# Seven block products instead of eight in the gate and up projections of a two-layer encoder

## The chip, the cores and the metric

The kernel runs on one core of a Trainium2 chip. The metric is the device time of one execution in microseconds (us), and three executions of the kernel before gave 2786.99, 2788.01 and 2792.45 us, so the median is 2788.01 us. A core has a matrix engine (TensorE, in the rows PE, with its weight loads as PEld), three engines for elementwise work (VectorE or DVE, ScalarE or ACT, GpSimd or POOL) and a queue that issues transfers (SyncE or SP).

## The reference

The program computes two layers on 1024 prompt tokens and 64 sample tokens, which the kernel treats as one block of 1088 tokens of width 1024. Layer 0 mixes tokens by attention and a gated recurrence, layer 1 by a convolution and a linear recurrence. Each layer ends with the same feed-forward network, and it is this network that the change touches:

```python
hn = (rms_norm(x, norm_ffn[l]) * (1.0 + sc2) + sh2).astype(x.dtype)
x = x + ((1.0 + g2) * swiglu(hn, ffn_wg[l], ffn_wu[l], ffn_wd[l])).astype(x.dtype)

def swiglu(h, wg, wu, wd):
    return (jax.nn.silu(h @ wg) * (h @ wu)) @ wd      # 1024 -> 2816 -> 1024
```

`sh2`, `sc2` and `g2` are rows of a matrix product of the conditioning vector with `w_ada` (six rows of 1024 for each layer).

## The kernel before

Features lie on partitions: `x` is 8 tiles of 128 features by 1088 tokens. Every float32 operand of a large product is split into a rounded part `hi` and a remainder `lo` (`split`, L85: ScalarE copies, VectorE or GpSimd subtracts), and a product is the sum of three passes hi·hi, hi·lo and lo·hi. Tokens come in three chunks of 384, 384 and 320 (`CH`).

The feed-forward (`ffn`, L319) runs over 22 blocks of 128 hidden features. For each it multiplies with the gate block and the up block: 8 tiles of K, 3 passes and 3 chunks, so 72 matmuls for each of the two (`gemm_chunk`, L108). ScalarE takes silu of the gate from PSUM, VectorE multiplies it with the up sum (L341), and the result is split and stays on chip. After every two blocks `project` (L300) multiplies them with their rows of `wd` and adds the gated sum into `x` (L313). Gate, up and down products thus alternate, and weights of 128x1024 are loaded and split two at a time through the pool `wp`, which exists for the whole program.

RMSNorm with its shift and scale (`norm_stats`, `norm_apply`, L240 to L276) for the feed-forward is made chunk by chunk behind the last output projection of the mixer (`norm_into`, called `after` chunks of `project`), reads the inverse root from PSUM and leaves `x` as it is. Five of the six conditioning rows of layer 0 are made during the mixer; row 5 of layer 0 and all of layer 1, 56 tiles, are made inside the feed-forward of layer 0 by `ada_tick`, on VectorE, GpSimd and ScalarE (`mods_dve`, L179). In layer 1 the last projection is `finish` (L1116), with the final norm in it.

Where code isn't under an `InOrder` wrapper (all operations of which show line 46), the order on each engine is made by the framework's planner, with `soon()` and `later()` as priorities; a pool's memory is handed on tile by tile (`reuse_waits="tile"`).

## Time and profile before

| | |
|---|---|
| median of three runs | 2788.01 us (2786.99 to 2792.45) |
| profiled execution, first to last instruction | 2788.7 us, 0.7 us above the median |
| PE busy | 2668.2 us, 96% |
| DVE, POOL, ACT busy | 1604.6, 1085.1, 921.5 us (58%, 39%, 33%) |
| feed-forward of layer 0 and 1 begin at about | 826 us and 1970 us |
| transfers | 193.78 MB, 69 GB/s over the span |

The profile is of one execution. Matmuls are pipelined, so that the duration of one is a latency and the rate is read from the distance of the starts. Where a row has "idle before", the engine named after the arrow is what ended the wait.

### The profile page before, as it was taken

To read this page: it belongs to the slowest core of one execution; us is meant where nothing else is said; L and a number is where in the kernel's file an instruction comes from. 1 tells how busy PE (TensorE), PEld (TensorE's weight loads), DVE (VectorE), ACT (ScalarE), POOL (GpSimd) and SP (SyncE) were. 2 spreads that over 40 slices of the span, in tenths; PEclk is the share of its full clock that TensorE was granted. 3 is DMA by queue.
4 is the path that set the end of the run, shared out by engine and by line. 5 is a ranking of instruction groups with operands and counts; after the bars stand their busy time and mean duration, and the time that the engine had idled before them with its cause. 6 is when DMAs were issued, how large, how long until landed. Compare 5 with 4: busy or idle time off the path is not lost.

```text
span 2788.7 us, 39952 instructions
## 1 busy us (share of the span) xinstructions
PE 2668.2 (96%) x16280; PEld 2611.0 (94%) x16280; DVE 1604.6 (58%) x2586; ACT 921.5 (33%) x1712; POOL 1085.1 (39%) x681
## 2 busy tenths in 40 slices
PE   6898999998899999999999999989999999999998
PEld 5898999998789999999999988989999999999997
DVE  8778766667985656643333476678633333333335
ACT  4225344444645333321111165553511111111113
POOL 6446445454645666621222254452512222222223
PEclk9999999999999999999999999999999999999999
DMA  6332111112213444411111102221001111111111
GB/s 241 91 109 89 58 40 55 41 61 106 66 46 121 134 135 130 135 55 46 46 46 41 50 28 73 68 89 48 22 31 46 46 46 46 46 46 46 46 46 65
DMA packets 69399, 193.78 MB, mean 69 GB/s; under 512 B 13280, under 2 KB 24544, under 8 KB 69216
## 3 DMA queue, kind: packets, MB, share of 16 engines
q1 hardware_dynamic: 69216, 191.24, 21.5%
q8 instruction: 128, 2.10, 0.3%
q14 instruction: 55, 0.45, 0.0%
HBM read 173.94 MB, written 17.27 MB: 69 GB/s over the span
## 4 chain that ended last, share of the span: by engine, by line
PE 48%; DVE 8%; ACT 4%; POOL 1%; issue 1%; DVEq 0%; POOLq 0%; ACTq 0%
PE ps_mm L115 29%; PE ps_z L308 8%; PE ps_t L308 8%; DVE xc L46 2%; POOL ada_raw L182 1%; DVE rg L46 1%; DVE mu L46 1%; PE ps_mm L308 1%; DVE junk L185 1%; DVE x L313 1%; ACT rg L46 1%; ACT mu L46 1%; ACT junk L183 1%; PE ps_t L46 0%; PE ps_t L115 0%
## 5 line engine op out<-in xcount | busy, mean ns | idle before, releaser
L115 PE MATMUL ps_mm<-h_hi,w_hi 128*128 128x384 f32 (+1 forms) x2688 | 885.5, 330 | 7.6 <-ACT w_hi L86 3.3
L115 PE MATMUL ps_mm<-h_hi,w_lo 128*128 128x384 f32 (+1 forms) x2688 | 886.5, 330 | 3.6 <-DVE w_lo L87 1.9
L115 PE MATMUL ps_mm<-h_lo,w_hi 128*128 128x384 f32 (+1 forms) x2688 | 886.5, 330 | 1.8 <-DVE h_lo L272 1.1
L87 POOL TENSOR_TENSOR w_lo<-w_raw,w_hi 128x1024 fp32r<-128x1024 f32 x168 | 427.2, 2546 | 1064.8 <-ACT w_hi L86 1012.1
L115 PEld LDWEIGHTS ps_mm<-h_hi,w_hi 128*128 128x128 f32 x2688 | 508.6, 189 | 12.1 <-ACT w_hi L86 4.1
L115 PEld LDWEIGHTS ps_mm<-h_hi,w_lo 128*128 128x128 f32 x2688 | 509.1, 189 | 5.8 <-DVE w_lo L87 2.2
L115 PEld LDWEIGHTS ps_mm<-h_lo,w_hi 128*128 128x128 f32 x2688 | 508.9, 189 | 3.5 <-DVE h_lo L272 1.4
L341 DVE TENSOR_TENSOR sg<-sg,ps_mm 128x384 f32<-128x384 f32 (+1 forms) x128 | 68.0, 531 | 502.5 <-PE ps_mm L115 496.6
L86 ACT CAST w_hi<-w_raw 128x1024 fp32r<-128x1024 f32 x174 | 181.7, 1049 | 276.5 <-PE ps_mm L115 198.0
L313 DVE SCALAR_TENSOR_TENSOR x<-ps_t,mods,x 128x384 f32<-128x384 f32 (+2 forms) x392 | 187.4, 498 | 124.5 <-PE ps_t L308 123.8
L308 PE MATMUL ps_z<-hid,w_hi 128*128 128x384 f32 (+1 forms) x1008 | 247.2, 327 | 0.3 <-DVE x L313 0.3
L308 PE MATMUL ps_t<-hid,w_hi 128*128 128x384 f32 (+1 forms) x1008 | 246.9, 327 | 0.0
L334 ACT ACTIVATE sg<-ps_mm 128x384 f32<-128x384 f32 (+1 forms) x128 | 60.3, 471 | 558.8 <-PE ps_mm L115 558.7
L313 DVE SCALAR_TENSOR_TENSOR x<-ps_z,mods,x 128x384 f32<-128x384 f32 (+2 forms) x396 | 187.4, 494 | 79.8 <-PE ps_z L308 79.5
L87 DVE TENSOR_TENSOR hid<-sg,hid 128x384 fp32r<-128x384 f32 x132 | 179.1, 1358 | 65.3 <-ACT hid L86 64.9
L308 PEld LDWEIGHTS ps_z<-hid,w_hi 128*128 128x128 f32 x1008 | 178.9, 188 | 0.8 <-DVE x L313 0.8
L308 PEld LDWEIGHTS ps_t<-hid,w_hi 128*128 128x128 f32 x1008 | 178.3, 188 | 0.0
L182 POOL TENSOR_TENSOR ada_raw<-ada_raw,cbc 128x1024 f32<-128x1024 f32 x56 | 137.2, 2450 | 92.1 <-DVE junk L185 53.8
L308 PE MATMUL ps_t<-hid,w_lo 128*128 128x384 f32 (+1 forms) x504 | 164.7, 327 | 0.0
L308 PE MATMUL ps_z<-hid,w_lo 128*128 128x384 f32 (+1 forms) x504 | 164.7, 327 | 0.0
L86 ACT CAST hid<-sg 128x384 fp32r<-128x384 f32 x132 | 65.1, 494 | 242.3 <-DVE sg L341 242.2
L185 DVE SCALAR_TENSOR_TENSOR junk<-ada_raw,cbc 128x1024 bf16<-128x1024 f32 x56 | 80.0, 1429 | 89.0 <-ACT junk L183 88.9
(389 smaller groups left out, 4593.7 us busy)
## 6 DMA issues: line engine op xcount, KB each, us to landing
ada_raw<-in_adaT SPq DMA_DIRECT2D x56, 512.0 KB, 3.5
w_raw<-in_wg SPq DMA_DIRECT2D x44, 512.0 KB, 3.6
w_raw<-in_wu SPq DMA_DIRECT2D x44, 512.0 KB, 3.5
w_raw<-in_wd SPq DMA_DIRECT2D x44, 512.0 KB, 3.5
w_raw<-in_w_in_even SPq DMA_DIRECT2D x28, 512.0 KB, 3.7
w_raw<-in_adaT SPq DMA_DIRECT2D x24, 512.0 KB, 3.6
w_raw<-in_w_in_odd SPq DMA_DIRECT2D x16, 512.0 KB, 3.6
o_raw<-o_dram SPq DMA_DIRECT2D x14, 544.0 KB, 3.9
```

Source lines behind the costliest of these rows:

```text
L46: return lambda *a, **k: self.tc.keep_in_program_order(f(*a, **k))
L86: S.copy(hi, src)
L87: (lo_eng or G).tensor_sub(lo, src, hi.bitcast(F32))
L115: PE.matmul(ps[:, :n], a[:, k * P:(k + 1) * P], b[:, c0:c0 + n], start=(i == 0), stop=(i == last))
L182: G.tensor_mul(raw, raw, cb[v])
L183: S.activation(junk(), raw, AF.Identity, accum_out=mods[l][:, t, v:v + 1])
L185: V.scalar_tensor_tensor(junk(), raw, 1.0, cb[v], ALU.mult, ALU.mult, accum_out=mods[l][:, t, v:v + 1])
L308: PE.matmul(ps[:, :n], a[:, m * P:(m + 1) * P], b[:, c0:c0 + n], start=(i == 0), stop=(i == 3 * nk - 1))
L313: V.scalar_tensor_tensor(x[m][:, r0:r0 + rn], ps[:, r0 - c0:r0 - c0 + rn], gate[:, m, b:b + 1], x[m][:, r0:r0 + rn], ALU.mult, ALU.add)
L334: S.activation(sg[ci][:, :n], ps, AF.Silu)
L341: V.tensor_mul(t, t, ps)
```

## The change

For a block of 128 hidden features the weights are seen as a 2x2 matrix of blocks: w11 and w12 are the gate's lower and upper half of K (512 each), w21 and w22 the up projection's. The activations are a 2x2 matrix too: lower and upper half of K by the first and second 544 tokens. Seven products of such blocks (each 4 tiles of K, 3 passes, 2 chunks of 272 tokens) with sums and differences of blocks ahead of and behind them give the four blocks of the result. The seven operands of the activations are made once for a layer (`enter`: `first_ops` and `late_ops`), the sums of the weights for each of the 22 blocks (`weights`).

For these operands to fit, `x` is written to DRAM before it is normalised in place, and read back after the 22 blocks (`unpark`). The hidden blocks go to DRAM one by one and come back in `down_half`, where the down projections run by groups of 2 or 3 blocks after all gate and up products. Conditioning row 5 of layer 0 is made on TensorE in the mixer (`todo_pe`); the 48 tiles of layer 1 are made during the down projections of layer 0. The last output projection of a mixer runs in four chunks of 272 tokens. The pools `wp` and `w2` and the PSUM pool are opened anew for each stage. The core of the diff:

```diff
+HT = NT // 2
+Q = HT // 2
+CH4 = [(0, Q), (HT, Q), (Q, Q), (HT + Q, Q)]
...
+    def enter(l, x, tag, stat_tmp, tmp):
+        ops = [[] for _ in range(7)]
+        def late_ops(j):
+            A, B = slice(j * Q, (j + 1) * Q), slice(HT + j * Q, HT + (j + 1) * Q)
+            for k in range(4):
+                split_at(x[k + 4][:, A], ops[4][k], j, G)
+            for k in range(4):
+                V.tensor_sub(x[k + 4][:, A], x[k + 4][:, A], x[k][:, A])
+                split_at(x[k + 4][:, A], ops[5][k], j, V)
+            for k in range(4):
+                d, c = x[k + 4][:, B], slice(j * Q, (j + 1) * Q)
+                hi, lo = ops[6][k][:, 0, c], ops[6][k][:, 1, c]
+                S.activation(hi, d, AF.Copy, scale=-1.0)
+                V.scalar_tensor_tensor(lo, d, -1.0, hi.bitcast(F32), ALU.mult, ALU.subtract)
+        def first_ops(j):
...
+            for k in range(4):
+                split_at(x[k][:, A], ops[0][k], j, V)
+            for k in range(4):
+                a, b, d = x[k][:, A], x[k][:, B], x[k + 4][:, B]
+                t1 = tmp()[:, :Q]
+                V.tensor_sub(t1, b, a)
+                V.tensor_sub(b, b, d)
+                V.tensor_sub(a, a, b)
+                split_at(a, ops[1][k], j, V)
+                split_at(b, ops[2][k], j, G)
+                split_at(t1, ops[3][k], j, G)
+        def after(ci):
+            c0, n = CH4[ci]
+            r = slice(c0, c0 + n)
+            for k in range(KD):
+                dma(x_dram[k][:, r], x[k][:, r])
+            rs = norm_stats(CH4[ci], x, stat_tmp)
+            kept = tmp()[:, :n]
+            S.copy(kept, rs)
+            for k in range(KD):
+                (G if k in (2, 3, 7) else V).tensor_mul(x[k][:, r], x[k][:, r], kept)
+                for r0, rn, b in rng(c0, n):
+                    v = x[k][:, r0:r0 + rn]
+                    S.activation(v, v, AF.Identity, scale=scale[l][1][:, k, b:b + 1], bias=mods[l][:, 3 * KD + k, b:b + 1])
+            if ci % 2:
+                first_ops(ci // 2)
+        return (ops, late_ops), after
+    def up_half(l, ops_late, t_tag, op_tag):
...
+            layout(fp, ("n22", NT, 4), ("t4", NT, 4), ("b21", NT, 4), ("wg", 1024, 2), ("wu", 1024, 2), ("s1", 512, 1),
+                   ("wh", 512, 5), ("wl", 512, 5))
+            def w_split(src):
...
+                split(src, hi, lo, G)
+                return hi, lo
+            def weights(f):
...
+                with soon():
+                    yield w_split(w11)
+                    V.tensor_add(s1, w21, w22)
+                    V.tensor_add(w21, w11, w21)
+                    V.tensor_add(w11, s1, w11)
+                    yield w_split(w11)
+                    yield w_split(w21)
+                    yield w_split(s1)
+                    yield w_split(w12)
+                    V.tensor_add(w12, w11, w12)
+                    yield w_split(w22)
+                    yield w_split(w12)
+            with soon():
...
+                late_ops(0)
+                late_ops(1)
...
+                for f in range(FF):
+                    X, Y, Z, W = (ap.tile([P, 2, 512], F32, name="acc" + n, tag="acc" + n, bufs=1) for n in "XYZW")
...
+                    def n1():
+                        S.copy(t, x_)
+                    def n6():
+                        V.tensor_sub(t, y_, t)
+                    def p7():
+                        V.tensor_add(hB, z_, t)
+                    def n5():
+                        V.tensor_add(hB, w_, hB)
+                    def n2():
+                        S.activation(g, x_, AF.Silu)
+                    def p4():
+                        V.tensor_add(hA, z_, t)
+                        V.tensor_mul(hA, hA, g)
+                        dma(hid_dram[f][:, :HT], hid[:, :HT])
+                    def p3():
+                        V.tensor_add(t, w_, t)
+                        S.activation(t, t, AF.Silu, scale=-1.0)
+                        V.tensor_mul(hB, hB, t)
+                        dma(hid_dram[f][:, HT:], hid[:, HT:])
+                    steps = list(zip((X, Y, Z, W, X, Z, W), ops, (1, 1, 1, 1, 0, 0, 0), (n1, n6, p7, n5, n2, p4, p3)))
+                    ws = weights(f)
+                    for part in ((steps[:4], steps[4:]) if f == 0 else [[st] for st in steps]):
+                        wt = [next(ws) for _ in part]
+                        for j in range(2):
+                            for w, (acc, op, start, use) in zip(wt, part):
+                                product(acc, w, op, j, start)
+                                if j == 1:
+                                    with soon():
+                                        use()
...
+    GROUPS = (2, 3, 3, 3, 3, 3, 3, 2)
+    def down_half(l, x, fp, t_tag, after=None, last=None, tick=None):
...
+                dma(lo.bitcast(F32), hid_dram[f])
+                with soon():
+                    split(lo.bitcast(F32), hi, lo, V)
+                hs.append((hi, lo))
+                ws.append(load_w(I["wd"][l, f], fp, "wd", bufs=6))
...
+                project(ws, hs, x, mod(l, 5), after if gi == len(GROUPS) - 1 else tick, ("t", "z", "mm"))
...
+                if not todo and todo_pe:
+                    j = todo_pe.pop(0)
+                    raw = raw_tile()
+                    dma(raw, I["ada5"][j])
+                    ps = bank("o")
+                    for e in range(KD):
+                        PE.matmul(ps[:, :2], raw[:, e * P:(e + 1) * P], sc[:, e, :], start=(e == 0), stop=(e == KD - 1))
...
+        todo = [(i, j) for i in range(6) for j in range(KD)]
+        def ada_tick(ci):
+            with later():
+                for n in range(3 if len(todo) > 24 else 2):
...
+                    mods_dve(1, i * KD + j, cb, raw,
+                             lambda: fp.tile([P, 1024], BF16, name="junk", tag="junk"), j % 2 == 0)
```

## Rows read from the trace of the kernel before

**Rows 1.** The page's first part: busy time, share of the span, instructions.

```profile
span 2788.7 us, 39952 instructions
PE 2668.2 (96%) x16280; PEld 2611.0 (94%) x16280; DVE 1604.6 (58%) x2586; ACT 921.5 (33%) x1712; POOL 1085.1 (39%) x681
```

**Rows 2.** Windows: stretch, its length, busy time of PE, PEld, DVE, ACT, POOL; granted clock.

```profile
300.00:500.00 200.00, 197.52 (x1330) 189.43 (x1330) 131.32 (x187) 86.77 (x198) 97.98 (x79) 0.99 0.15 45
...
860.00:1050.00 190.00, 189.86 (x1153) 189.54 (x1152) 111.33 (x171) 72.12 (x118) 118.30 (x48) 1.00 0.45 140
...
2155.00:2724.00 569.00, 569.00 (x3446) 569.00 (x3445) 208.18 (x350) 93.71 (x144) 116.45 (x48) 1.00 0.15 45
```

**Rows 3.** Windows over the two entries: last output projection and first feed-forward block.

```profile
1943.50:2007.50 64.00, 59.55 (x331) 58.16 (x330) 48.62 (x100) 36.22 (x76) 31.53 (x33) 0.89 0.05 17
798.30:855.50 57.20, 52.41 (x304) 50.68 (x305) 47.30 (x96) 34.61 (x75) 36.04 (x36) 0.94 0.16 54
```

**Rows 4.** Chain that ended last, layer 1: start us, us, what.

```profile
2155.45 34.20 PE ps_mm L115 x208
2190.16 7.68 PE ps_mm L115 x48
2226.80 34.20 PE ps_mm L115 x208
```

**Rows 5.** Timeline of PE: the first matmul of three runs of 24.

```profile
2308.46 0.33 PE L115 MATMUL ps_mm<-h_hi,w_hi 128*128 128x384 f32 x1
...
2312.62 0.31 PE L115 MATMUL ps_mm<-h_hi,w_hi 128*128 128x320 f32 x1
...
2316.13 0.34 PE L115 MATMUL ps_mm<-h_hi,w_hi 128*128 128x384 f32 x1
```

**Rows 6.** Timeline of PE in the last projection, 256 columns, 30 matmuls apart.

```profile
2765.94 0.40 PE L46 MATMUL ps_z<-hid,w_hi 128*128 128x256 f32 x2
...
2769.44 0.40 PE L46 MATMUL ps_t<-hid,w_hi 128*128 128x256 f32 x2
```

**Rows 7.** Groups of DVE, feed-forward of layer 1, 2084 to 2724 us.

```profile
L313 DVE SCALAR_TENSOR_TENSOR x<-ps_t,mods,x 128x384 f32<-128x384 f32 x72 | 44.3, 616 | 39.1 <-PE ps_t L308 38.9
...
L87 DVE TENSOR_TENSOR hid<-sg,hid 128x320 fp32r<-128x320 f32 x18 | 43.8, 2433 | 9.5 <-ACT hid L86 9.5
L341 DVE TENSOR_TENSOR sg<-sg,ps_mm 128x384 f32<-128x384 f32 x36 | 20.0, 555 | 247.7 <-PE ps_mm L115 247.7
L313 DVE SCALAR_TENSOR_TENSOR x<-ps_z,mods,x 128x256 f32<-128x256 f32 x35 | 16.9, 484 | 10.1 <-PE ps_z L308 10.1
...
L313 DVE SCALAR_TENSOR_TENSOR x<-ps_t,mods,x 128x64 f32<-128x64 f32 x36 | 9.9, 275 | 0.0
```

**Rows 8.** Groups of POOL and of ACT in the same stretch.

```profile
L87 POOL TENSOR_TENSOR w_lo<-w_raw,w_hi 128x1024 fp32r<-128x1024 f32 x54 | 131.0, 2430 | 510.4 <-ACT w_hi L86 510.3
...
L86 ACT CAST w_hi<-w_raw 128x1024 fp32r<-128x1024 f32 x54 | 56.7, 1050 | 116.1 <-PE ps_mm L115 92.7 <-DMA w_raw<-in_wd 23.4
```

**Rows 9.** Timeline of DVE and of POOL in the entry to layer 1's feed-forward.

```profile
1949.75 0.55 DVE L251 TENSOR_TENSOR ntmp<-ntmp 128x384 f32<-128x384 f32 x1
...
1952.33 0.94 DVE L251 TENSOR_TENSOR ntmp<-ntmp 128x384 f32<-128x384 f32 x1
...
1981.63 0.48 DVE L251 TENSOR_TENSOR ntmp<-ntmp 128x320 f32<-128x320 f32 x1
...
1994.60 2.42 DVE L268 SCALAR_TENSOR_TENSOR ntmp<-x,scale,ps_o 128x256 f32<-128x256 f32 x8 [4.23 <-PE ps_o L230]
...
1952.03 0.83 POOL L248 TENSOR_TENSOR ntmp<-x 128x384 f32<-128x384 f32 x1 [0.29 <-DVE x L313]
...
1967.22 1.01 POOL L253 TENSOR_TENSOR ntmp<-ntmp 128x384 f32<-128x384 f32 x1 [1.62 <-DVE ntmp L251]
```

**Rows 10.** Groups of DVE in that entry, 1943.5 to 2007.5 us.

```profile
L251 DVE TENSOR_TENSOR ntmp<-ntmp 128x384 f32<-128x384 f32 x8 | 5.5, 685 | 0.1
...
L251 DVE TENSOR_TENSOR ntmp<-ntmp 128x320 f32<-128x320 f32 x4 | 3.7, 923 | 0.0
```

**Rows 11.** Timeline of PE in the first mixer: the 16 conditioning products of one tile.

```profile
68.23 1.84 PE L46 MATMUL ps_o<-sc,raw_sc 128*128 128x2 f32 x16
```

**Rows 12.** Groups of DVE in the feed-forward of layer 0, 860 to 1222 us.

```profile
L185 DVE SCALAR_TENSOR_TENSOR junk<-ada_raw,cbc 128x1024 bf16<-128x1024 f32 x56 | 80.0, 1429 | 89.0 <-ACT junk L183 88.9
L87 DVE TENSOR_TENSOR hid<-sg,hid 128x384 fp32r<-128x384 f32 x22 | 35.6, 1618 | 7.5 <-ACT hid L86 7.2
```

**Rows 13.** DMA issues of the page: KB of each, median us from issue to landing.

```profile
w_raw<-in_wd SPq DMA_DIRECT2D x44, 512.0 KB, 3.5
...
o_raw<-o_dram SPq DMA_DIRECT2D x14, 544.0 KB, 3.9
```

More of the change, by code (lines that the diff above doesn't have):

```diff
@@ new lines, in unpark @@
+    def unpark(tag):
+        x = [u(tag, name="x") for _ in range(KD)]
+        for c0, n in CH:
+            for k in range(KD):
+                dma(x[k][:, c0:c0 + n], x_dram[k][:, c0:c0 + n])
+        return x
+    GROUPS = (2, 3, 3, 3, 3, 3, 3, 2)
+    def down_half(l, x, fp, t_tag, after=None, last=None, tick=None):
+        f = 0
+        for gi, size in enumerate(GROUPS):
+            hs, ws = [], []
+            for f in range(f, f + size):
+                if gi == len(GROUPS) - 1:
+                    t = fp.tile([P, 2, NT], F32R, name="hid", tag="hid", bufs=2)
+                    hi, lo = t[:, 0, :], t[:, 1, :]
+                else:
+                    tag = t_tag if f < 2 or f % 2 else "C"
+                    hi, lo = u(tag, F32R, "hid_hi"), u(tag, F32R, "hid_lo")
+                dma(lo.bitcast(F32), hid_dram[f])
[3 more added lines that the diff above has]
+                ws.append(load_w(I["wd"][l, f], fp, "wd", bufs=6))
+            f += 1
+            if gi == len(GROUPS) - 1 and last:
+                last(ws, hs)
+            else:
+                project(ws, hs, x, mod(l, 5), after if gi == len(GROUPS) - 1 else tick, ("t", "z", "mm"))
@@ L366, in hybrid_encoder @@
     o_dram = [dram.tile([P, NT], F32, name=f"o_dram{k}") for k in range(KD)]
+    x_dram = [dram.tile([P, NT], F32, name=f"x_dram{k}") for k in range(KD)]
+    hid_dram = [dram.tile([P, NT], F32, name=f"hid_dram{f}") for f in range(FF)]
     wi = I["w_in_even"]
-    with phase_pool("mix") as mp:
+    banks_open = psum_pool("banks0")
+    with phase_pool("wp") as stage["w"], phase_pool("mix") as mp:
+        masks = mp.tile([P, 6, P], U8, name="masks")
+        causal = mp.tile([P, P], F32, name="causal")
+        strict = mp.tile([P, P], F32, name="strict")
@@ L515, in hybrid_encoder @@
         for i in range(2):
-            w = tuple(wp.tile([P, 1024], F32R, name=nm, tag=nm, bufs=2) for nm in ("w_hi", "w_lo"))
+            w = tuple(stage["w"].tile([P, 1024], F32R, name=nm, tag=nm, bufs=2) for nm in ("w_hi", "w_lo"))
             oS.copy(w[0], wraw[i])
@@ L1049, in bring, with odd_out @@
             outs[j] = hi, lo
-        def odd_out(js, own, aft=None):
+        def odd_out(js, own, aft=None, chunks=CH):
             for j in js:
                 if j not in outs:
-                    bring(j, lambda name, dt=F32: u("A" if name == "o_raw" else "C", dt, name), G)
+                    bring(j, lambda name, dt=F32: u("B" if name == "o_raw" else "C", dt, name), G)
             hs = [outs[j] for j in js]
@@ L1232, in hybrid_encoder @@
         POOL_Y = ((0, 2, 4), (5,), (0, 3, 6))
-        ffn(1, x, box[0], fp, None, 0, 1, finish)
+        x = unpark("B")
+        down_half(1, x, fp, "A", last=finish)
+    stage["open"].close()
 def _layout(i):
```

215 lines of the change are left out of this document (104 added, 111 removed).

## The prediction

> **What bounds the kernel now.** I read the page first, for the share of each engine, then windows by stage, the chain that ended last, the timeline of PE for its rate, the groups of the elementwise engines inside one stage, and last the two places where a mixer hands over to the feed-forward. PE is busy 96% of 2788.7 us [rows 1]. In both feed-forwards it has no gap: 569.00 of 569.00 us in layer 1, at full granted clock (1.00, which is the 2.4 GHz level) [rows 2]. The chain of layer 1 runs on PE alone and repeats every 71.35 us (2155.45 to 2226.80), two hidden blocks with their down products [rows 4]. The reader is to see that in these stages only fewer or shorter matmuls shorten anything: DVE is busy 208 of 569 us, POOL 116 [rows 2]. At the two entries it is otherwise: 64.0 us pass with 59.55 of PE and a clock of 0.89, and 57.2 us with 52.41 and 0.94, while DVE is busy 76% and 83% of them [rows 3].
>
> **The change, part by part.** The sum is made against the profiled execution, 2788.7 us, which is 0.7 us above the median of the runs; I leave that difference in.
>
> *Gate and up products.* A matmul of 384 columns starts 4.16/24 = 0.1733 us after the one before, one of 320 columns 3.51/24 = 0.1463 [rows 5]. One block now is 144 matmuls: 24 x 2 x (2 x 0.1733 + 0.1463) = 23.66 us; two of them and two blocks of down products make 71.0 of the 71.35 seen. After the change it is 7 products x 4 tiles x 3 passes x 2 halves = 168 matmuls of 272 columns. No row has 272. The line through 384 and 320 gives 0.1260; between 320 and the 256 columns of the last projection (30 starts in 3.50 us, 0.1167 [rows 6]) it is 0.1241. I take 0.125: 21.0 us a block. The gain is 2.66 us for each of 44 blocks, 117 us; the ends are 2.49 and 2.81, 110 and 124 us. An eighth of the columns goes, but not an eighth of the time, because 24 more matmuls a block each bring the part that does not go with columns. The row of 256 is 10 ns above 256 columns at 2.4 GHz, those of 320 and 384 are 13 ns above [rows 5, 6]. The Trainium skill (TensorE: Matmul & The Clock Gate, "Wait — 56ns, not 53.3ns?") has 2.5 ns for this part; by it a matmul of 272 would take 115.8 ns, an estimate, and the gain would be larger than mine by 1.5 us a block. These rows show four to five times that, and the measurement decides.
>
> *What must stay behind those products.* A product lasts 3.0 us, a block 21. POOL makes seven remainders of 512 columns, half of 2430 ns each [rows 8]: 8.5 us. ACT has seven copies at half of 1050 ns and three passes of 544 columns: some 6 us. DVE has four sums of 512, near 0.65, and seven passes of 544, near 0.72 (from 0.555 at 384 [rows 7]): 7.6 us, and more by waits for POOL: a subtraction of 320 columns with both inputs in SBUF takes 2433 ns where POOL works, as long as POOL's own 2430 [rows 7, 8]. Six such operations a block with half a POOL operation each add 4 us. All are far under 21, and an accumulator is read at least two products (6 us) before it is written again. So I put the steady state at PE's rate, plus 0.1 us a block for hand-overs, 4 us. If this cover were gone, the next to bind would be DVE.
>
> *The two entries.* This is where I expect most of the gain to go. Before, PE starts on chunk 0 while the norm of later chunks is made. After, the first four products need two of four chunks, the rest all of them, and the elementwise work is larger. For 272 columns I take DVE 0.43 us with two SBUF inputs (0.48 and 0.55 at 320 and 384 [rows 9]), 0.50 from PSUM (0.484 at 256 [rows 7]), POOL 0.64 to 0.75 (0.83 and 1.01 at 384 [rows 9]). DVE for each chunk: 8 additions into x 4.0 (5.6 in the last chunk, whose 208 + 64 columns are two operations, 275 ns at 64 [rows 7]), 5 sums and 5 multiplications 4.3, the power's input 0.15; over four chunks 35.6. `first_ops`: 20 operations twice, 17.2. `late_ops`: 12 twice, 10.4. Together 63 us without a wait, against 48.6 before with waits [rows 3]. Of these 104 have two SBUF inputs and meet POOL, which by its rows has 41 us of its own here and up to 9 more for the weights of block 0. In the entry before, such operations took 685 ns and 923 ns instead of 550 and 480 [rows 9, 10], 0.24 us more at the mean of these twelve. That puts 25 us on DVE; without it DVE has 63, with all of it 88. I take 80, and 3 us for the norm's latency (an idle DVE of 4.23 us stands before the last chunk [rows 9]), 5 for the products left when the last operand comes and 2 for a lower clock: 90 us from the first matmul of the last projection to the end of block 0. The ends are 69 (63, 1 and 5) and 105 (88, 4, 5, and 8 for the clock). Before it was 64.0 and 57.2 [rows 3]; less the 2.7 already counted, 61.3 and 54.5. So the entries cost 29 and 35 more, 64 us in all (22 to 95, and 10 more if the first weights of layer 0 too, whose memory the mixer's last temporaries hold, come late by the load, the copy and the remainder of two, [rows 8, 13]). PE has 45 us of work in such a stretch, so it must idle some 40 us and its clock fall; those at 0.89 and 0.94 [rows 3] show a milder form.
>
> *Conditioning on PE.* A tile's 16 small products take 1.84 us [rows 11], of which the last's tail is hidden by the next matmul; I take 1.75, and eight are 14 us. The mixer's PE is busy 197.5 of 200 us in one stretch [rows 2], so little is hidden: 10 us (4 to 14).
>
> *Hand-overs.* From up to down, weights of the first group wait for memory of the last products: a load of 3.5 us [rows 13] is ahead of time, a remainder of 2.4 us [rows 8] is not; x and hidden blocks (3.9 us for 544 KB [rows 13]) have products in flight as cover. I take 3 us, twice (0 to 6 each). From down to the second mixer the first weights no longer lie in a pool of their own: 3.5 + 1.05 + 2.4 less the norm's tail, 5 us (0 to 8).
>
> *Down projections of layer 0.* PE has 22 x 11.83 = 260 us here. DVE has additions into x, 24 in each of 8 groups, 15.8 us a group, 126; remainders of 22 hidden blocks, 26 clean or up to 55 (1618 ns for 384 in rows where POOL shares [rows 12]); 72 conditioning dots at 1.43 us [rows 12], 103; and three norm chunks at the end. That is 255 to 285 us before the norm. Before, the same dots had 720 us to lie in. Evictions go first, so PE isn't stopped at once, but the rest becomes late and holds the memory and the start of the second mixer. I take 12 us (0 to 35). The down products themselves stay as they are; layer 1 has no dots and hides its remainders.
>
> Sum: -117 + 64 + 10 + 6 + 5 + 12 + 4 = -16 us; 2788.7 - 16 gives 2773 us.
>
> **The rivals.**
> 1. *The entry is mostly hidden.* For it: late operands are asked for early, DVE can work through the last projection, and the planner may pack DVE and POOL apart. Then the entries cost 22 to 35, the down stage little: 2788.7 - 117 + 28 + 20 = 2720, range 2700 to 2745. Against it: DVE is already busy 76 and 83% of the shorter entries.
> 2. *DVE binds outside the products* (slower). Both entries at 105, and the dots of the down stage pushed into the second mixer: -117 + 95 + 14 + 10 + 8 + 30 + 4 = +44, near 2833. It decides from about 80 us of entry cost together with 20 of the down stage. For it: the sums above reach it without a mishap when every SBUF operation waits as it did. Against it: operations that follow on each other on DVE shut POOL out just as well.
> 3. *No gain from seven products.* PE's rate could be set by weight loads, of which there are 168 now for 144, or by the operand chain. If a matmul of 272 took the 0.1463 of 320, a block would take 24.6 us and the time would go up by 40 before all else: 2880. Against it: 256 columns ran at 0.1167, so loads keep that pace [rows 6]. The Trainium skill (the same page, "LDWEIGHTS (loading the stationary operand)") puts a load of 128 columns at 107 ns, an estimate that stays under 125; by that the rate holds.
>
> **How the numbers follow.** Two runs differ by up to 0.2%, so 2782.4 to 2793.6 us is no change. My own case, entry costs between 45 and 85 us, has 0.46, and gives 2745 to 2795; rival 1 has 0.21; rival 2 has 0.28; rival 3 has 0.05. Faster is rival 1 and most of my case: 0.60. Same is the upper end of mine and the lower edge of rival 2: 0.11. Slower: 0.29. The range runs from rival 1's lower end to where rival 2's upper part is cut: 2703 to 2825. My own case alone is 2745 to 2795.
>
> **What would show it.** Right: groups of 168 matmuls a block at 0.124 to 0.126 us distance without gaps, blocks every 21 us; two idle stretches of PE of 30 us or more where DVE waits on POOL; the granted clock at half there. Wrong: blocks slower than 21.5 us with PE waiting for `wl` or an accumulator; or an entry under 70 us; or dots still running when the second mixer begins, with PE waiting for x in the down stage.

## The result, and the profile after

The changed kernel takes 2861.43 us (median of 4 runs, 2852.45 to 2864.79) against 2789.53 on the same chip: a ratio of 1.0248, 95% interval 1.0229 to 1.0266. It is slower by 72 us; 2773 us with 0.60 for faster was wrong, and the range (to 2825) missed it. The profiled execution took 2864.79 us with a span of 2863.0, 74.3 us more than before.

The windows of the changed kernel, in the columns of [rows 2]: the first mixer, the entry to layer 0's up stage (from the first matmul of the last output projection to the end of block 0), the part of it between that projection and the first product, the up stage, the down stage, and the entry of layer 1.

```profile
300.00:500.00 200.00, 193.90 (x1209) 184.30 (x1208) 113.53 (x171) 77.37 (x174) 86.84 (x70) 0.89 0.18 56
831.90:936.60 104.70, 60.27 (x411) 56.61 (x412) 86.52 (x161) 58.39 (x140) 66.27 (x69) 0.76 0.23 77
862.50:904.20 41.70, 6.58 (x29) 5.63 (x27) 38.96 (x71) 32.16 (x82) 30.96 (x33) 0.53 0.17 55
925.00:1377.60 452.60, 452.60 (x3620) 452.42 (x3619) 188.30 (x234) 129.78 (x214) 198.70 (x148) 1.00 0.28 86
1390.00:1680.00 290.00, 272.28 (x1603) 267.73 (x1604) 258.26 (x449) 77.58 (x109) 130.79 (x59) 0.97 0.48 161
2021.10:2124.30 103.20, 59.09 (x418) 56.95 (x418) 84.77 (x162) 55.83 (x136) 63.88 (x66) 0.75 0.21 74
```

The fourth line is what the change is for, and it does it: 3620 matmuls in 452.60 us of which PE is busy 452.60, 0.1250 us each, 21.0 us for the 168 of a block. The other lines are what it costs. The entries were 57.2 and 64.0 us [rows 3] and are 104.7 and 103.2; for 41.7 us of the first PE has 6.6 us of work, DVE 39.0, and the granted clock is 0.53, just above the lower level of 1.2 GHz. The mixer runs at 0.89 where it ran at 0.99 [rows 2].

The waits of PE in the changed kernel (waiting matmul, what ended the wait: us in all, times, longest):

```profile
PE ps_o L239 <- POOL r L232: 36.2, 10, 8.4
PE accX L431 <- ACT wh L98: 33.6, 2, 16.8
PE ps_t L311 <- ACT w_hi L98: 23.7, 3, 12.7
PE ps_o L223 <- DVE ntmp L261: 20.6, 6, 8.3
...
PE accX L431 <- POOL wl L99: 12.7, 2, 6.4
```

Nearly all of these waits lie at the seams: the last norms (lines 223 and 239), the weights of block 0 (`wh`, `wl`), and the first down weights (`w_hi`). None lies inside the steady products.

Where the 74.3 us are, by stretches of the two profiled executions. Borders of before are those of [rows 3] and 1620.8 us, where the second mixer's products begin (the last six down products still follow, about 1 us); those of after 831.9, 936.6, 1670.8, 2021.1 and 2124.3, block 0's end counted back from the last product by 21 blocks of 21.0. Counted by its 144 matmuls, the first block of layer 0 ended at 858.5 us before, not at the 855.5 of [rows 3], so the second row is 3 us too large and the third 3 us too small. In the last column each term of the prediction stands in its stretch.

| stretch | before, us | after, us | difference | predicted |
|---|---|---|---|---|
| start to the last projection, layer 0 | 798.3 | 831.9 | +33.6 | +10 |
| entry, layer 0 | 57.2 | 104.7 | +47.5 | +32 |
| blocks 1 to 21 and all down products, layer 0 | 765.3 | 734.2 | -31.1 | -39 |
| second mixer, to its last projection | 322.7 | 350.3 | +27.6 | +5 |
| entry, layer 1 | 64.0 | 103.2 | +39.2 | +26 |
| the rest | 781.2 | 738.7 | -42.5 | -51 |

### The profile page after: what moved, and what is told of

Its sections match the earlier page's. It is cut to its first block, busy times and chain, and to the rows that moved or that the text cites. A ratio compares the mean times of both kernels' runs of the same rounds, so it can differ in the third digit from the quotient of the medians.

```text
span 2863.0 us, 44449 instructions
## 1 busy us (share of the span) xinstructions
PE 2610.7 (91%) x17584; PEld 2549.8 (89%) x17584; DVE 1814.2 (63%) x2806; ACT 1026.6 (36%) x1891; POOL 1269.6 (44%) x923
## 4 chain that ended last, share of the span: by engine, by line
PE 60%; DVE 22%; DMA 5%; ACT 5%; issue 4%; POOL 4%; SPq 0%; DVEq 0%; POOLq 0%; ACTq 0%
PE accZ L431 9%; PE accX L431 9%; PE accW L431 9%; PE ps_mm L127 7%; PE ps_mm L311 5%; PE accY L431 5%; PE ps_t L311 4%; PE ps_z L311 4%; DVE junk L194 3%; DVE x L316 3%; DVE xc L51 2%; DMA w_raw<-in_adaT 1%; DVE om L779 1%; PE ps_z L882 1%; PE ps_z L770 1%
## 5 line engine op out<-in xcount | busy, mean ns | idle before, releaser
L99 POOL TENSOR_TENSOR wl<-wg,wh 128x512 fp32r<-128x512 f32 x176 | 228.3, 1297 | 225.8 <-ACT wh L98 225.1
L431 PE MATMUL accX<-op,wh 128*128 128x272 f32 x1408 | 275.0, 291 | 33.6 <-ACT wh L98 33.6
L431 PE MATMUL accW<-op,wh 128*128 128x272 f32 x1408 | 274.4, 287 | 0.0
L431 PE MATMUL accZ<-op,wh 128*128 128x272 f32 x1408 | 271.1, 287 | 0.0
L431 PEld LDWEIGHTS accX<-op,wh 128*128 128x128 f32 x1408 | 224.1, 191 | 34.2 <-ACT wh L98 34.2
L127 PE MATMUL ps_mm<-h_hi,w_hi 128*128 128x384 f32 (+1 forms) x640 | 219.6, 343 | 11.2 <-ACT w_hi L98 9.9
L431 PEld LDWEIGHTS accW<-op,wh 128*128 128x128 f32 x1408 | 223.2, 188 | 0.4 <-ACT wh L98 0.4
L431 PEld LDWEIGHTS accZ<-op,wh 128*128 128x128 f32 x1408 | 220.8, 188 | 0.4 <-ACT wh L98 0.4
L127 PE MATMUL ps_mm<-h_hi,w_lo 128*128 128x384 f32 (+1 forms) x640 | 218.0, 342 | 2.0 <-POOL w_lo L99 2.0
L127 PE MATMUL ps_mm<-h_lo,w_hi 128*128 128x384 f32 (+1 forms) x640 | 217.7, 340 | 0.0
```

Source lines behind the costliest of these rows:

```text
L99: (lo_eng or G).tensor_sub(lo, src, hi.bitcast(F32))
L127: PE.matmul(ps[:, :n], a[:, k * P:(k + 1) * P], b[:, c0:c0 + n], start=(i == 0), stop=(i == last))
L431: PE.matmul(acc[:, j, :Q], a[:, k * P:(k + 1) * P], op[k][:, b, c], start=(start == 1 and i == 0), stop=(i == 11), skip_group_check=True)
```

## The experiments

Theory, after the two traces: the products gain what was predicted; the loss sits in five seams, and in each of them VectorE or an order of instructions holds TensorE up. The runs take the seams one by one. "The first product" is counted from the first matmul of the last projection (72.3 and 70.9 us in the changed kernel), "the third block" to ScalarE's Silu over the accumulator of block 2 (141.1 and 139.6 us), which also sees how block 0 ends, as long as the products of a block keep their order. Where the planner changed that order (e5 and e10), the end of block 0 is counted instead, as the time by which 168 up products have begun (104.4 and 103.0 us). Most runs were taken once, and the same unedited stage differs by up to 14 us between them, so stages are compared rather than totals.

**e1, row 5 of layer 0's conditioning back on VectorE.**

```diff
-        todo = [(i, j) for i in (2, 3, 4) for j in range(KD)]
-        todo_pe = list(range(KD))
+        todo = [(i, j) for i in (2, 3, 4, 5) for j in range(KD)]
+        todo_pe = []
```

> Row 5 of layer 0's conditioning goes from TensorE to the way of rows 2 to 4 (two dots a tile on VectorE, in the mixer). In the changed kernel the first matmul of the last output projection starts at 831.9 us, before at 798.3. Theory: the 128 small matmuls of row 5 made this, 14 us by themselves and as much again because the granted clock falls around them (0.89 in 300 to 500 us, before 0.99). Then that start goes back to 805 us (797 to 815) and the time falls by 18 to 35 us. Rival: the pools that are now opened and handed on stage by stage slow the mixer. Then the start stays above 825 us, the clock stays low, and the time changes by less than 8 us.

2836.96 us. The last projection starts at 808.2 us instead of 831.9: 23.7 us, and no stage behind it moves by more than 3 us. The window of e1's mixer shows the clock back at 0.97:

```profile
300.00:500.00 200.00, 188.18 (x1251) 178.88 (x1250) 146.68 (x210) 82.18 (x190) 97.91 (x79) 0.97 0.20 61
```

The eight tiles' 128 products of two columns cost more than the 14 us forecast for them, and the clock is lower while they are there; how much of the 24 is the clock the run doesn't separate. In other runs that leave this stage alone the same start lay between 824 and 838 us, so 24 is good to some 7. It isn't all that row 5 costs: before, the row was made in the feed-forward, and here it is made in the mixer on VectorE, which is busy 147 us of this window for 131 before. Where it left the mixer altogether (e6, e7, e9, e11) the last projection started at 791 to 800 us, and the window is that of before again. e6:

```profile
300.00:500.00 200.00, 197.51 (x1329) 189.42 (x1329) 131.10 (x187) 86.79 (x198) 97.85 (x79) 0.99 0.15 45
```

**e2, weights of the first block asked for ahead of the late entries.**

```diff
+            ws = weights(0)
+            wt0 = [next(ws) for _ in range(4)]
             with soon():
...
                 late_ops(0)
                 late_ops(1)
```

> The four weight blocks that hidden block 0 needs first are asked for ahead of the late operands of the entry; nothing else is changed. In the changed kernel the first product of each layer waits 16.8 us for the rounded weights and then 6.4 us for the remainder on GpSimd, behind 11 subtractions of late operands. Theory: the order on ScalarE and GpSimd cost these last microseconds, and the operands themselves are there: the wait for the remainder goes and the first product starts 3 to 6 us earlier, so 8 to 12 us at each entry and 16 to 24 us in all. Rival: the operands' own work on VectorE sets the entry; then products wait for operands in place of weights and the time changes by less than 6 us.

2855.43 us; the first product came 72.1 and 70.8 us after the projection's start, as before the edit, with the same waits of 16.8 and 6.4 us. Asking earlier didn't place the casts earlier, so this run says nothing on the order.

**e3, without layer 1's 48 conditioning tiles in the down stage** (layer 1's modulation is zero).

```diff
-                    raw = fp.tile([P, 1024], F32, name="ada_raw", tag="ada_raw", bufs=2)
-                    dma(raw, I["adaT"][48 + i * KD + j])
-                    mods_dve(1, i * KD + j, cb, raw,
-                             lambda: fp.tile([P, 1024], BF16, name="junk", tag="junk"), j % 2 == 0)
```

> The 48 conditioning tiles of layer 1 are left out (their transfers, products and dots; zeros stand for them, so layer 1 is computed with the biases alone). Theory: the dots fill VectorE in the down projections of layer 0 (258 of 290 us busy) and make the norm behind them late. Then the stretch from the first down product to the last falls from 281 to 262 to 270 us, the gap from the last down product (1671) to the first product of the second mixer (1704) falls from 33 to below 18 us, and the time falls by 25 to 40 us. Rival: that gap is set by the first weights of the second mixer, whose rounding stands last on ScalarE; then it stays above 25 us and the time falls by less than 20 us.

2835.06 us. The down stage went from 280.5 to 266.0 us, the gap behind it from 33.4 to 26.4. The dots cost 14.5 us there and 7 in the gap; 26 us of gap have another cause, so the theory's number for the gap (below 18) failed. Inside the stage the dots hold up the evictions: TensorE's waits for them in the changed kernel, then in e3:

```profile
PE ps_t L311 <- DVE x L316: 4.1, 4, 1.8
PE ps_z L311 <- DVE x L316: 3.5, 4, 1.8
PE ps_mm L311 <- DVE x L316: 3.2, 2, 2.2
```

```profile
PE ps_t L313 <- DVE x L318: 1.2, 2, 0.7
```

**e4, the entries' work on GpSimd moved to VectorE and ScalarE.**

```diff
-            if e in (1, 2):
+            if sq and e in (1, 2):
...
-                (G if k in (2, 3, 7) else V).tensor_mul(x[k][:, r], x[k][:, r], kept)
+                V.tensor_mul(x[k][:, r], x[k][:, r], kept)
...
-                split_at(b, ops[2][k], j, G)
+                split_at(b, ops[2][k], j, V)
```

> All of GpSimd's work in the two entries but the power goes elsewhere: 8 squares to ScalarE, 8 sums, 12 multiplications and 24 subtractions to VectorE, for each layer. Theory: VectorE and GpSimd shut each other out there (an operation of 272 columns takes 0.95 us on either while both work, 0.43 on VectorE alone), so 44 operations at 0.35 to 0.43 us on VectorE cost less than their 0.95 on GpSimd: each entry gets shorter by 5 to 15 us, in all 10 to 30. Rival: the engines work side by side and VectorE binds by its own work; then it has 17 us more in each entry and the time goes up by 20 to 35 us.

2860.45 us; the first product after 70.6 and 70.1 us. Neither number came. The groups of VectorE between projection and first product tell why: the first two lines are the changed kernel, the next two e4 (busy us, mean ns of one).

```profile
L376 DVE TENSOR_TENSOR x<-x,ntmp 128x272 f32<-128x272 f32 x15 | 11.3, 808 | 1.1 <-ACT ntmp L374 1.1
L99 DVE TENSOR_TENSOR op<-x,op 128x272 fp32r<-128x272 f32 x12 | 8.3, 752 | 0.0
```

```profile
L99 DVE TENSOR_TENSOR op<-x,op 128x272 fp32r<-128x272 f32 x28 | 11.0, 438 | 1.8 <-ACT op L98 1.8
L376 DVE TENSOR_TENSOR x<-x,ntmp 128x272 f32<-128x272 f32 x19 | 7.0, 435 | 2.9 <-ACT ntmp L374 2.9
```

One operation takes about 437 ns in e4, where GpSimd is nearly quiet, and about 780 beside GpSimd. To the first product VectorE did 175 instructions in 63.1 us where it had done 131 in 66.2, with GpSimd busy 9.8 us instead of 48.4. For this work the two engines are one: what GpSimd does, VectorE pays for in full, and a division of the work between them gains nothing.

**e5, the last chunk's norm put behind the opening of the up stage's memory**, weights and late entries asked for ahead of it.

```diff
+            ws = weights(0)
+            wt0 = [next(ws) for _ in range(4)]
             with soon():
...
+                after(3, fp)
                 late_ops(0)
                 late_ops(1)
```

> The changed kernel with the norm of the last chunk of the last output projection moved behind the opening of the up stage's memory (its temporaries lie there), the first block's weights and the late entries asked for ahead of it, and, in layer 0, the weights' buffers on memory that is free early. Nothing else moves. Theory (the entry is long because weights and late entries stand in their engines' queues behind the last norm, while TensorE has nothing to do): the first product starts at the spread of the last norm, some 55 us after the start of the last projection instead of 72, the later entries are there in time, and each layer's entry loses 20 to 30 us: 2800 to 2825 us. Rival (the chain through the last norm itself sets the time, the order of what stands behind it doesn't matter): under 8 us for each layer, 2845 to 2861 us.

2900.99 us, slower by 40. The Silu of the third block came 6 us earlier in each layer (135.0 and 133.3), but only because the planner put the products of a block in another order; counted, block 0 ended at 104.3 and 102.7 us, where it did without the edit. The up products of layer 0 from the start of the last projection, in the changed kernel, in e5 and in e10 below (stretch, its length, busy time and number of matmuls, clock):

```profile
831.90:936.30 104.40, 24.92 (x168) 0.75 0.23 77
829.70:934.00 104.30, 27.75 (x168) 0.75 0.22 77
831.90:940.50 108.60, 33.45 (x168) 0.75 0.21 74
```

The first products began 3 us earlier (68.9 and 67.7) and then waited for late entries. From there a block took 22.0 us instead of 21.0, TensorE waiting 0.4 us for a split weight in most, and 6.6 us for evictions in the last one of layer 0; the up stages' products ended 27 and 26 us later. The edit also put the buffers of `wg` and `wu` into one ring; which part of it changed the order of the products and splits was not separated.

**e6, all dots of row 5 and layer 1 in layer 0's up stage**, where VectorE has 264 of 452.6 us free. To make room, the remainders of the split weights (`wl`) have four buffers instead of five, in both layers.

```diff
+                for n in range(3):
...
+                    raw = fp.tile([P, 1024], F32, name="ada_raw", tag="ada_raw", bufs=1)
+                    dma(raw, I["adaT"][l * 48 + i * KD + j])
+                    mods_dve(l, i * KD + j, tick.cb, raw,
```

> The changed kernel with row 5 of layer 0's conditioning and all 48 tiles of layer 1's on VectorE in layer 0's up stage, where VectorE was busy 188 of 453 us; none in the mixer and none in the down stage. Theory (row 5 cost 24 us on TensorE, the 48 tiles 14.5 us in the down stage and 7 in the gap behind it, and VectorE has some 260 us to spare in the up stage): mixer 800 to 808 us, down stage of layer 0 266, gap 26, block period still 20.63 us; 2808 to 2820 us. Rival (VectorE's dots delay the evictions of the products, TensorE waits for accumulators): the block period of layer 0 rises to 21.5 us or more, which gives back 18 us or more: 2830 us or more.

2880.63 us. Mixer 795.5, down stage 265.4, gap 26.4 as the theory has them, but blocks of layer 0 took 21.4 to 28.0 us while dots lay in them. Group of the dots on VectorE in that stage, then TensorE's waits in it:

```profile
L194 DVE SCALAR_TENSOR_TENSOR junk<-ada_raw,cbc 128x1024 bf16<-128x1024 f32 x93 | 144.2, 1550 | 81.3 <-DMA ada_raw<-in_adaT 80.8
```

```profile
PE accZ L432 <- DVE hid L450: 30.4, 12, 4.6
```

VectorE stood 80.8 us waiting for a tile's transfer (one buffer), with the evictions of the products queued behind the waiting dot. The rival's price came, more by a wait than by a want of time.

**e7, e5 and e6 together**, four buffers for the split weights.

> Both edits of the two runs before together (four buffers instead of five for the split weights, to make room). If their gains add up (theory): 2861 - 24 - 22 - 40 to 60 us, 2755 to 2780 us, faster than before the change. Rival (they share idle time, or the products wait for weights with four buffers): 2790 us or more.

2907.23 us, ratio 1.0415 (1.0398 to 1.0432): the rival. In layer 1, where no dots lie, a block took 21.8 us. e5's edit alone made it 22.0, so this run doesn't show what four buffers cost; e9 does.

**e8, without the late entries** (products 5 to 7 of each block read the first operands instead).

```diff
-                    ops[o] = [halves(fp.tile([P, NT], F32R, name="op", tag=tag, bufs=4)) for _ in range(4)]
-                late_ops(0)
-                late_ops(1)
+                    ops[o] = ops[o - 4]
```

> The changed kernel with the late entries (operands 4 to 6, made of the second halves of the channels) left out and the first products' operands read in their place, so the up products of blocks are not the reference's; all products, their timing and everything else stay. Left out in each layer: 24 operations on VectorE, 24 on ScalarE, 8 on GpSimd, all between the end of the last output projection and the end of block 0. Theory (the entry lasts as long as VectorE and GpSimd need for the elementwise work that stands between the projection and the first products; VectorE was busy 39 of 41.7 us there): the entry of each layer loses 12 to 25 us, 2812 to 2837 us. Rival (the chain through the last chunk's norm sets the entry; the late entries run beside it): less than 6 us for each layer, 2849 to 2861 us.

2846.32 us. The third block came after 130.4 and 130.9 us: 10.7 and 8.7 us less, between the two numbers. 24 operations on VectorE at e4's 438 ns are 10.5 us; beside GpSimd in the changed kernel they took some 15, in part beside the first products. The entry loses about what they cost at the former price, and less than the theory's 12 to 25. Even without them VectorE was busy 62 of the 68 us to the first product.

**e13, without the sums of the last norm** in each entry (the scale of the chunk before is used).

```diff
+            if ci < 3:
                 rs = norm_stats(CH4[ci], x, stat_tmp)
                 kept = tmp()[:, :n]
                 S.copy(kept, rs)
+                box[:] = [kept]
+            kept = box[0]
```

> The changed kernel without the norm's sums of the last chunk before each up stage: the scale of the chunk before is used again, so the outputs of those 272 columns are not the reference's. Left out in each layer: 3 operations on VectorE, 5 on GpSimd (one of them the power), 7 on ScalarE and 6 small matmuls; all entries are still made. Theory of volume (VectorE and GpSimd are busy without a break from the end of the projection to the first product): the entry loses what these take, 2 to 6 us for each layer, 2849 to 2858 us. Rival (the chain sums, power, spread, copy is what the first product waits for): 12 us or more for each layer, 2838 us or less.

2854.39 us; the third block after 137.7 and 136.1 us, 3.4 and 3.5 us earlier. The chain of sums, power, spread and copy is gone, and TensorE waits as long, only for something else; its first wait of e13:

```profile
PE accX L435 <- ACT wh L98: 58.2, 2, 29.1
```

The first product came only 1.5 us earlier (70.8 and 69.5), so the rival is out. With e4 and e8: up to the first product the entry is as long as VectorE and GpSimd need, and the names on TensorE's waits only say what came last.

**e10, e5 with its order written out**: sums of the norm, weights, late entries of the first half, the rest of the norm, entries of the second half.

```diff
+                tail = last(fp)
+                next(tail)
+            ws = weights(0)
+            wt0 = [next(ws) for _ in range(4)]
...
                 late_ops(0)
+                next(tail)
                 late_ops(1)
```

> As e5 (norm of the last chunk behind the opening of the up stage's memory), but with its order written out: sums of the norm first, then the first block's weights and the late entries of the first half of the columns, then the rest of the norm, then the entries of the second half. Theory of volume (VectorE and GpSimd together are the entry's limit; order only decides which part of TensorE's first 20 us lies beside them): the first product starts 50 to 58 us after the start of the last projection instead of 72, block 0's end comes 5 to 12 us earlier in each layer, 2837 to 2852 us. Rival (order alone made the entry long): 20 us or more for each layer, 2820 us or less. If the spread of the last norm still comes at 54 us and the end of block 0 doesn't move, neither order nor overlap matters: 2855 us or more.

2885.83 us. The first product came at 66.1 and 64.9 us, but block 0 ended at 108.6 and 109.0 (104.4 and 103.0; the third row above). An earlier start of the products didn't bring an earlier end: the numbers of theory and rival both failed, and the last sentence of the expectation is nearest, though the spread of the last norm moved too, from 54 to 65 us in layer 0. Layer 1's blocks went to 22.0 us again, layer 0's stayed at 21.0.

**e9, the dots of e6 with two buffers and an order of VectorE**: at most one tile between two evictions. The split weights have four buffers instead of five for both halves, in both layers.

```diff
-                    def n6():
-                        V.tensor_sub(t, y_, t)
+                    def n6():
+                        uV.tensor_sub(t, y_, t)
...
+                                    if side and use in (p7, n2, p3):
+                                        side(f, (p7, n2, p3).index(use))
```

> Again row 5 and the 48 tiles of layer 1 on VectorE in layer 0's up stage, as in the run e6, but with two buffers for the tiles instead of one, the next load asked for before it is needed, and at most two dots of one tile between two evictions (an order written out for VectorE in this stage). Theory (e6's blocks grew to 26 us because VectorE stood waiting for a tile's transfer with the evictions of the products behind it, 80 us in 17 blocks, and not because it lacked time): block period back to 21.0 to 21.5 us; mixer 800 to 808, down stage 266, gap 26: 2795 to 2820 us. Rival (VectorE's own time is short: 17 us of eviction and weights and 9 us of dots in a block of 21 us, with GpSimd on the same port): block period 23 us or more, 2850 us or more.

2873.25 us. Blocks between 21.4 and 26.3 us, some 23.5 at the mean, on the rival's side. Group of the dots:

```profile
L51 DVE SCALAR_TENSOR_TENSOR junk<-ada_raw,cbc 128x1024 bf16<-128x1024 f32 x102 | 157.2, 1541 | 49.1 <-DMA ada_raw<-in_adaT 48.2
```

VectorE still waits 48 us for transfers, and is busy 315 of 420. Both theories hold in part; two buffers weren't enough to tell them apart. The four buffers have a part of their own: layer 1 has nothing else of this edit, and its blocks took 21.8 us. Its up products in 420 us of steady state, in the changed kernel and in e9:

```profile
2145.00:2565.00 420.00, 420.00 (x3361) 1.00 0.28 86
2135.00:2555.00 420.00, 413.08 (x3237) 1.00 0.23 77
```

From the first up product to the last it took 26 us more there than in the changed kernel, layer 0 55 more. If the buffers cost the same in both, the dots cost 29, and without the buffers' share the run would come to some 2822 us, an estimate: still slower than before the change.

**e11, e9 and e10 together.**

> Both edits of the two runs before together, with four buffers instead of five for the split weights. If the parts add up: row 5 -24, layer 1's dots -20, entries -10 to -20, hand-overs -5: 2790 to 2805 us, the same as before the change within 0.5%. If VectorE is short in the up stage: 2840 us or more.

2882.01 us, ratio 1.0333 (1.0316 to 1.0350): the second number. A block took 21.8 us in layer 1 and about 23 in layer 0.

**e12, the norm of the down stage's last chunk moved behind the loads of the second mixer's first weights.** The rows are TensorE's timeline between the last down product and the first product of the mixer, the changed kernel first, then e12.

```diff
+        first = load_x(0, S), load_g(0, S)
+        after2(2, slots(gp, "un", 12, 4, 2))
-        gemm_group([(load_x(0, S), x_to(ts_[0], S)), (load_g(0, S), g_to(ts_[0], S))], h)
+        gemm_group([(first[0], x_to(ts_[0], S)), (first[1], g_to(ts_[0], S))], h)
```

> The changed kernel with the norm of layer 1's last chunk of columns taken out of the down stage and put behind the loads of the second mixer's first two weights, with its temporaries on the mixer's memory; nothing else moves. Theory (the 33 us between the last down product and the second mixer's first product are a wait for two weights whose loads and casts stand behind that norm, because the mixer's memory can only be opened after it; the first two chunks of columns are ready long before): the gap falls to 10 to 22 us, 2840 to 2852 us. Rival (VectorE is behind with evictions and dots at that point and would be the limit in any order): 28 us or more of gap, 2855 us or more.

```profile
1670.81 0.31 PE L311 MATMUL ps_mm<-hid,w_lo 128*128 128x320 f32 x1
...
1679.76 1.65 PE L239 MATMUL ps_o<-ident,r 128*128 128x128 f32 x6 [5.00 <-POOL r L232]
1689.71 1.44 PE L223 MATMUL ps_o<-ones,ntmp 128*128 128x1 f32 x6 [8.31 <-DVE ntmp L261]
...
1704.25 0.69 PE L127 MATMUL ps_mm<-h_hi,w_hi 128*128 128x384 f32 x1 [8.98 <-ACT w_hi L98]
```

```profile
1665.93 0.31 PE L314 MATMUL ps_mm<-hid,w_lo 128*128 128x320 f32 x1
...
1674.89 1.65 PE L239 MATMUL ps_o<-ident,r 128*128 128x128 f32 x6 [5.28 <-POOL r L232]
1687.14 0.69 PE L127 MATMUL ps_mm<-h_hi,w_hi 128*128 128x384 f32 x1 [10.61 <-ACT w_hi L98]
```

2850.33 us. The gap fell from 33.4 to 21.2 us, the theory's number: the last norm's sums (the row at 1689.71) no longer stand ahead of the product. But the mixer behind took 324.4 us instead of 316.8, so 4.6 of the 12 us are left (the other runs without this edit lay between 316.8 and 318.5, e14 at 324.3). The norm has moved into the mixer, which presumably pays for it there; no run shows it.

**e14, e1 and e12 together**, the best of what the runs pointed to.

> The edits of the runs e1 and e12 together, the best of what the runs pointed to with every output computed: 2861 - 24 - 10 to 20 us if both add up, 2815 to 2828 us, still slower than before the change, since the entries stay. Rival (the two edits share idle time): 2830 us or more.

2829.34 us, ratio 1.0144 (1.0127 to 1.0161), between the two numbers. No version tried comes down to the kernel before.

## Why the prediction was wrong

*Gate and up products: right.* 0.125 us a matmul was forecast and 0.1250 measured, 21.0 us a block for 23.66, 117 us in all. Rival 3 is out. What the Trainium skill (TensorE: Matmul & The Clock Gate, "Wait — 56ns, not 53.3ns?") gives beside the columns, 2.5 ns, isn't what 272 columns show here: of 125.0 ns, 113.3 are the columns at 2.4 GHz and 11.7 are not.

*What must stay behind those products: right.* DVE was busy 188 of 452.6 us and POOL 199, and TensorE didn't wait. But that was no proof of slack. Dots (e6, e9), four buffers for the weights (layer 1 of e9), or the edits of e5 and e10 each made TensorE wait. That a block has 21 us in which seven splits must pass ScalarE and GpSimd in step is my reading; no run takes it apart.

*The entries: the step that failed most,* 90 us forecast for each, 104.7 and 103.2 measured, 28 more in all. The step put 90 us as 80 of DVE and 10 behind. DVE was busy 86.5 and 84.8, close to the upper end of 88, and idle for 18.2 and 18.4, not 10: some 6 before the first product and 12 beside block 0. So 11 of the 28 us missed are elementwise time, and 17 are an overlap that didn't come: the step let 5 us of products lie behind the last operand, but all of block 0 came behind the first product at 72.3 and 70.9 us and took 32 us, 6.4 of them a wait for a remainder, with the granted clock at 0.50 for the first 12 us. The 80 instead of 88 had no row; what the prediction says against rival 2, that operations which follow on each other shut GpSimd out, e4 doesn't bear out: with 39 us of GpSimd's work moved to VectorE the entry was as long, so that work had been paid in full. An operation took 808 ns in the changed kernel and 435 in e4. The Trainium skill (SBUF — State Buffer, "Who interferes with whom") states that VectorE with two SBUF inputs and a GpSimd that reads SBUF contend, and the two durations agree. e8 and e13 show that less volume makes the entry shorter by about what is left out, e5 and e10 that order doesn't. That block 0's weights stand behind the late entries is in the trace too. ScalarE's and GpSimd's timelines of the changed kernel:

```profile
902.23 1.39 ACT L347 ACTIVATE op<-x 128x272 fp32r<-128x272 f32 x4
903.52 0.61 ACT L98 CAST wh<-wg 128x512 fp32r<-128x512 f32 x1
```

```profile
899.52 10.39 POOL L99 TENSOR_TENSOR op<-x,op 128x272 fp32r<-128x272 f32 x11
909.87 1.46 POOL L99 TENSOR_TENSOR wl<-wg,wh 128x512 fp32r<-128x512 f32 x1
```

The cast of the first weight comes after the late entries' casts, its remainder after a run of eleven, eight of them the late entries' (GpSimd has no more of these). The prediction had this as a possible 10 us for layer 0; e5 and e10, which put the weights ahead, brought the first product forward by 3 and 6 us and won nothing at the end of block 0.

*Conditioning on PE: failed.* 10 us (4 to 14) forecast, 33.6 measured up to the last projection. The step counted the products' time and took the rest of the mixer as it was; the clock fell from 0.99 to 0.89. Without row 5 in the mixer at all (e6, e9) that point came at 795.5 and 796.1 us, before it was 798.3, so the row is the whole of the loss: 24 us of it go when VectorE makes the row instead (e1), and some 10 are what VectorE's way costs in the mixer, which had no such work before.

*Hand-overs from up to down: failed,* 3 us each forecast; TensorE stood 12.66 and 10.46 us. What was late is not the remainder but the load. The changed kernel's timelines of SP, ScalarE and TensorE:

```profile
1380.07 0.32 SPq L460 DMA_DIRECT2D hid_dram<-hid  x1
...
1381.42 0.92 SPq L107 DMA_DIRECT2D w_raw<-in_wd  x2
```

```profile
1384.19 1.28 ACT L184 ACT_TABLE_LOAD   x1
...
1389.21 1.05 ACT L98 CAST w_hi<-w_raw 128x1024 fp32r<-128x1024 f32 x1
```

```profile
1390.31 0.69 PE L311 MATMUL ps_t<-hid_hi,w_hi 128*128 128x384 f32 x1 [12.66 <-ACT w_hi L98]
```

The weights' loads are issued 4 us after the last product, behind a store of the last hidden block, which waits for its eviction, and the cast of the first stands behind a table load and two sigmoids for the conditioning. Where these went to the up stage (e6, e9) layer 0's last matmul of the up stage and the first of the down stage lay 5.0 and 5.1 us apart. But there the loads were also issued ahead of the last product, by 3 us in e6 (1419.0 against 1422.1), and layer 1, which has no sigmoids, went from 10.8 to 5.2 in e6 and 6.6 in e9. In layer 1 of the changed kernel ScalarE itself waited 2.8 us for the load. So its issue is at least a large part; what the sigmoids cost was not separated, nor why the order changed.

*Down projections of layer 0: right in size, not in the way.* 12 us (0 to 35) were forecast, and the dots cost 14.5 in the stage and 7 behind it (e3). The step expected evictions to go first, and the loss at the start of the second mixer. But two thirds fell inside the stage, where TensorE waited 10.8 us for evictions behind dots, against 1.2 without them.

*Second mixer: failed,* 5 us forecast, 28 measured. The step counted the first weights; it left out that the last norm runs with TensorE idle, where before products of the last blocks lay beside it. The gap is 33.4 us, and the mixer behind it gives some 5 back (316.8 us from its first product, 322.3 before). Dots took 7 (e3); of e12's 12 only 4.6 stayed. Some 16 us are left to the norm and the first casts, shown by waits but by no run.

Together: 28 for the entries, 24 for row 5, 23 for the second mixer and 17 for the hand-overs, less the 4 us set aside for the steady state, which weren't needed, are nearly all of the 90 us between the -16 forecast and the +74 measured.

Of the rivals, the second (DVE binds outside the products, 2833 us) named the mechanism, and its entries of 105 us are what came. It was 28 us short, mainly by row 5 and the hand-overs. Its weight of 0.28 was too small: its condition, that SBUF operations wait as they did in [rows 9, 10], was what the trace of before had shown, and I priced between the ends instead.

## What to carry to other kernels

A scheme that saves products pays in sums, and those fall where the stages meet: price an entry by the elementwise engines' full volume, VectorE and GpSimd as one engine where both inputs lie in SBUF, and take what TensorE idles there as lost, with the granted clock near its lower level (0.53 here). Splitting an interleaved stage into two costs a seam each time (a load, a cast, a norm with nothing beside it), here TensorE stood 10 to 33 us. A stage in which TensorE is busy 100% isn't a place with room because another engine is idle in it: work that waits for a transfer holds up the evictions behind it.

## What the runs showed that was not expected

- Some 44 more instructions on VectorE, taken over from GpSimd, cost it no time: 175 in 63.1 us for 131 in 66.2 (e4).
- 128 matmuls of two columns, spread over 200 us of a mixer in which PE is busy 97%, went with a granted clock of 0.89; without them it was 0.97 (e1, with the row on VectorE) and 0.99 (e6, and before [rows 2]).
- The up stage at 21.0 us a block stands on an edge: four buffers instead of five for both halves of the split weights made it 21.8 (layer 1 of e9), the edits of e5 made it 22.0.
- Another order of the products in a block moved its Silu by 6 us while the block's end stayed (e5): an instruction in the middle of a block is no measure of the block.
